# Modulation vectors computed in pairs over four blocks of partitions, with tied steps, in a FoX/GLA trunk

## The chip, the cores and the metric

The kernel runs on one core of one Trainium2 chip. The metric is the device time of one execution in microseconds (us). Times of single executions are given as the median, lowest and highest of several runs. The profile comes from one execution of its own, whose time is given beside the others. Engines are TensorE (PE, with its weight loads as PEld), VectorE (DVE), ScalarE (ACT), GpSimd (POOL) and SyncE (SP), whose queue starts nearly all the DMAs.

## What is computed

The reference is a trunk of two layers on a sequence of 1024 tokens with 1024 channels. Layer 0 mixes tokens with forgetting attention (FoX, 16 heads of 64 channels, softmax with a cumulative log gate), layer 1 with gated linear attention (GLA, 4 heads, chunks with a decayed state). Each mixer is followed by a SwiGLU feed-forward network (FFN) of width 2816. Before each of these four parts the stream is normalized and modulated by vectors that come from one conditioning vector c:

```python
    c_act = jax.nn.silu(c)
    for i in range(DEPTH):
        mod = c_act @ ada_w[i] + ada_b[i]
        sh1, sc1, g1, sh2, sc2, g2 = jnp.split(mod, N_MOD, axis=-1)
        h = modulate(rms_norm(x, norm1_g[i]), sh1, sc1)
        ...
        x = x + g1[:, None, :] * y
        h = modulate(rms_norm(x, norm2_g[i]), sh2, sc2)
        x = x + g2[:, None, :] * swiglu(h, ffn_w_in[i], ffn_w_out[i])
    return rms_norm(x, final_g)
```

The change is about the line with `mod`: for each layer a row vector of 1024 numbers times a matrix of 1024 rows and 6144 columns, cut into six vectors j = 0 to 5 of 1024 numbers. All data is float32.

## The kernel before, in words

**Products.** Each large product is made of three matmuls on parts: every operand is split into a high part, rounded to a short float (fp32r), and the rest, and high*high, high*low and low*high are summed in PSUM (`mm3`, L237 to L239). `split` (L159, L160) makes the parts: ACT copies the high part, DVE subtracts it. Weights come in by 512 KB DMAs into a ring `wr` of three slots (L162) and are split from there (`load_w`, L193 to L206). A `Weights` object loads a fixed number of weight tiles ahead. The FFN uses products of sums of blocks (a Strassen scheme), with sums on POOL (L683, L685) and DVE (L1285), and spills to device memory through SP.

**Order.** The program is written as one stream of instructions with data dependencies. A scheduler of the framework then sets the order on each engine, by its own estimate of durations, so an instruction without a reason to wait may move ahead of instructions written before it. `tc.issue_after(i)` ties the instructions issued under it behind instruction i. `weave` interleaves two generators by their estimated work: the attention steps of one head pair (`attention`, with the softmax in L902 to L962) with the projections of the next pair (`qk_proj`, and `v_half` for the value projection, whose weights are the tiles wv and whose PSUM tiles are vps).

**Modulation before.** At the start, vectors 0 and 1 of layer 0 come in eight slices of 128 columns (`load_ada0`, `ada0_mod`, L455 to L474), partly by matmuls, partly by DVE (L470) and a final matmul with a column of ones (L472). They feed the first normalized blocks (`h_block`, L476 to L484). The change leaves these alone. All the other vectors come from `ada_steps` (L336 to L383), one vector j at a time. Eight row blocks of 128 rows of `ada_w` are multiplied by their 128 numbers of silu(c), one for each partition, and added into `acc`. Eight (or, for a half vector, four) matmuls with `ones` (L377) then sum over the partitions, each giving a column of 128 numbers, DVE adds the bias from `vec` into `modc` (L379), and `make_a` (L333) makes the scale of the norm.

- *Layer 0, vectors 2 to 5*: a load of 512 KB (128 rows by 1024 columns) per step goes through the ring `wr` (L345), and four DVE instructions of 256 columns scale and add it (L367 for the first row block, L369 for the others). These steps are paced by `ada0(3.0)` after each `qk_proj` (L879).
- *Layer 1, all vectors*: half vectors, a load of 256 KB per step, always one step ahead; ACT scales (L358 for the first, L360 for the others) and POOL adds (L361). Vectors 0 and 1 run in the FFN of layer 0, paced by `ada1(...)` after its products (L1280), the others in GLA (after `gv_body`, and after the projections in `head_front`). The pace sets how much other work is written between steps (`ADA_A`, `ADA_B`).

**GLA gates.** `gate_z`, `gate_sum` and `gate_exps` make the decay factors of a head: two small matmuls (L1596, L1597), activations, two scans over the tokens on DVE (L1610), and exponentials. `head_front` makes the k and q projections of one head (PSUM tiles gk and gqp) and in between takes the two steps of `gate_ahead`, the same chain for the next head. In every head the steps were taken after the two halves of the k projection.

Of the kernel before, what the change touches and what calls it, by code (L numbers as in the profile page):

```python
# [16 lines left out]
P = 128  # L17
# [36 lines left out]
def trunk(ctx, tc, x, c, ada_w, ada_b, norm1_g, norm2_g, ffn_w_in, ffn_w_out,  # L54
# [98 lines left out]
    mhalf = cst.tile([P, 8], F32, name="mhalf")  # L153
    nc.vector.memset(mhalf, -0.5)
    maskb = cst.tile([P, P], BF16, name="maskb")
    tri = cst.tile([P, P], I32, name="tri")
# [123 lines left out]
    def load_ada0(d):  # L280
        for kh in range(2):
# [3 lines left out]
            araw[(d, kh)] = t  # L285

    load_x(0)
    rows2 = mrows[1][0:32]
# [26 lines left out]
    cact = cst.tile([P, 8], F32, name="cact")  # L315
    nc.scalar.activation(cact, vps[:, P:P + 8], AF.Silu)
    nc.vector.tensor_copy(vec, vps)
    gocol = lambda k: vec[:, P + 8 + k: P + 9 + k]
# [16 lines left out]

    def ada_steps(l, j, acc_of, raw_of, w):  # L336

        steps = deque((c0, k) for c0 in range(0, D, w) for k in range(8))
        got = deque()

        def load():
            if steps:
                c0, k = steps.popleft()
                raw = raw_of([P, w], F32, f"ada{l}{j}{c0}{k}")
                nc.sync.dma_start(raw, ada_w[l, psl(k), j * D + c0:j * D + c0 + w])  # L345
                got.append(raw)

        for c0 in range(0, D, w):
            acc = acc_of([P, w], F32, f"acc{l}{j}{c0}")
            for k in range(8):  # L350
                if w == D or c0 == k == 0:
                    load()
                raw = got.popleft()
                if w < D:
                    load()
                    yield ADA_A
                    if k == 0:
                        nc.scalar.mul(acc, raw, cact[:, 0:1])  # L358
                    else:
                        nc.scalar.mul(raw, raw, cact[:, k:k + 1])  # L360
                        nc.gpsimd.tensor_add(acc, acc, raw)  # L361
                    yield ADA_B
                    continue
                for q in range(0, w, 256):
                    cs = slice(q, q + 256)
                    if k == 0:
                        nc.vector.tensor_scalar(acc[:, cs], raw[:, cs], cact[:, 0:1], None, op0=ALU.mult)  # L367
                    else:
                        nc.vector.scalar_tensor_tensor(acc[:, cs], raw[:, cs], cact[:, k:k + 1], acc[:, cs],  # L369
                                                       op0=ALU.mult, op1=ALU.add)  # L370
                yield 1.0
            if w < D:
                yield ADA_B
            n, b = w // P, c0 // P
            mp = pj([P, n], F32, f"mp{l}{j}{c0}")
            for k in range(n):
                nc.tensor.matmul(mp[:, k:k + 1], acc[:, psl(k)], ones, start=True, stop=True)  # L377
            o = l * 48 + j * 8 + b
            nc.vector.tensor_add(modc[:, l, j, b:b + n], mp, vec[:, o:o + n])  # L379
            for i, jj in ((0, 1), (1, 4)):  # L380
                if j == jj:
                    make_a(l, i, slice(b, b + n))
        yield 1.0  # L383
# [24 lines left out]

    def ada1_queue(js, acc, raws_, w):
        r = Cycle(raws_)  # L410
        for j in js:
            ada1.q.append(ada_steps(1, j, lambda *_: acc, r, w))

# [576 lines left out]

    for j in (2, 3, 4, 5):
        ada0.q.append(ada_steps(0, j, acc_r, wr, D))
    run(v_half(0, 1))
# [522 lines left out]
    def mid0():  # L1516
        v = Views(slots["hid"], 2, [HALF], "ad0").v
        ada1_queue((0, 1), v[0], v[1:4], HALF)

# [22 lines left out]
    ada_v = Views(take(2), 2, [HALF], "ad").v  # L1542
    ada1_queue((2, 3, 4, 5), ada_v[0], ada_v[1:3], HALF)
    ADA_A, ADA_B = 2.5, 1.0
# [100 lines left out]
    def head_front(h, b16, t2, ei, nmid):  # L1645
# [4 lines left out]
        for hf in range(2):  # L1650
            cs = hsl(hf)
            ps = pj([P, HALF], F32, f"gk{h}{hf}")
            run(proj(ps, wk, h1, hf))
            ada1(5.1)
            y = yv()
            nc.vector.tensor_mul(y, ps, ei[:, cs])
            nc.vector.tensor_mul(t2[:, cs], ps, t2[:, cs])
            split(kin.hi[:, cs], kin.lo[:, cs], y)
            for n in range(4 * hf, 4 * hf + 4):
                nc.scalar.activation(ei[:, psl(n)], b16[:, psl(n)], AF.Exp, scale=1.0 / 16, bias=nmid[:, n:n + 1])  # L1660
            nc.scalar.activation(b16[:, cs], b16[:, cs], AF.Exp, scale=1.0 / 16)
            next(ahead, None)
        wq = feed.next()
        qt = [Pair(qr([P, S], FR, f"gq{h}{i}h"), qr([P, S], FR, f"gq{h}{i}l")) for i in range(2)]
        for hf in range(2):
            cs = hsl(hf)
            ps = pj([P, HALF], F32, f"gqp{h}{hf}")
            run(proj(ps, wq, h1, hf))
            ada1(5.1)
            for t, f in zip(qt, (ei, b16)):  # L1670
                y = yv()
                nc.vector.scalar_tensor_tensor(y, ps, QS, f[:, cs], op0=ALU.mult, op1=ALU.mult)
                split(t.hi[:, cs], t.lo[:, cs], y)
        return kin, qt

# [241 lines left out]
```

## Time and profile before

| | us |
|---|---|
| runs, median | 2447.19 |
| runs, lowest and highest | 2445.64, 2450.05 |
| profiled execution | 2444.76 |
| its span | 2443.0 |

The granted clock of PE over the profiled execution is 0.993 of full. The page of the profile gives, for each engine, busy time and share of the span; the view of waits says which instruction waited for which engine's tile or DMA; the timeline lists single instructions with their start, duration and, in brackets, the idle time of the engine ahead of them and what ended it; windows give busy times by stretches. Names are the program's, with numbers left out: `mp` is the PSUM tile of the modulation sums, `ad` and `ada` tiles are rows of `ada_w` (for layer 1 and 0), `adas` the slices at the start, `acc` the sums.

### The profile page before, as it was taken

The page shows a single profiled execution, that of the slowest core. Times are in us where ns is not written, and L with a number is a line of the kernel's source. Part 1 is how long each engine was busy: PE and PEld are TensorE (multiplying, and loading weights), DVE is VectorE, ACT ScalarE, POOL GpSimd, SP SyncE. Part 2 cuts the span into 40 slices and gives each one's busy share as a digit, 9 for nine tenths or more (in the row PEclk, how much of TensorE's full clock was granted, in tenths as well). Part 3 has the DMA queues.
Part 4 walks back from the last instruction along what each step waited for, and adds up shares of the span by engine and source line. Part 5 has one row for each costly group of instructions (what it writes and reads, how often), then busy time and mean ns, then how long its engine had stood idle before and what let it go on. Part 6 is the DMA issues. An engine that isn't in the chain of part 4 may idle for free.

```text
span 2443.0 us, 35539 instructions
## 1 busy us (share of the span) xinstructions
PE 2384.9 (98%) x12458; PEld 2028.7 (83%) x12458; DVE 1703.0 (70%) x2849; ACT 1192.8 (49%) x2280; POOL 1151.1 (47%) x1006
## 2 busy tenths in 40 slices
PE   6999999999999999999999899999999999999998
PEld 5788888878887878888888798898888888888888
DVE  6477777776687768675788456546487667665787
ACT  4565665665554443435324756654344333335325
POOL 4233333333348776653363544442326656653362
PEclk9999999999999999999999999999999999999999
DMA  8224333233326544347665333435325434347664
GB/s 269 80 87 121 96 96 120 70 96 113 128 94 212 183 164 164 125 162 261 228 215 178 92 114 111 125 107 169 107 73 191 147 134 155 130 166 257 232 209 149
DMA packets 319067, 362.34 MB, mean 148 GB/s; under 512 B 18140, under 2 KB 246648, under 8 KB 318888
## 3 DMA queue, kind: packets, MB, share of 16 engines
q1 hardware_dynamic: 318888, 360.07, 44.2%
q8 instruction: 98, 1.61, 0.3%
q14 instruction: 81, 0.66, 0.1%
HBM read 269.76 MB, written 90.24 MB: 147 GB/s over the span
## 4 chain that ended last, share of the span: by engine, by line
PE 82%; DVE 7%; DMA 3%; ACT 3%; issue 3%; POOL 2%; SPq 0%; DVEq 0%; POOLq 0%; ACTq 0%
PE p_b L237 15%; PE p_b L239 15%; PE p_b L238 14%; PE o_b L947 2%; PE t_b L933 2%; PE qk_b L237 2%; PE qk_b L238 2%; PE qk_b L239 2%; DMA ad_s<-in_ada_w_dram 1%; PE s_b L902 1%; PE s_b L903 1%; PE gv_b L237 1%; PE gv_b L239 1%; PE gv_b L238 1%; PE vps_b L237 1%
## 5 line engine op out<-in xcount | busy, mean ns | idle before, releaser
L160 DVE TENSOR_TENSOR o_s<-xv_s,o_s 128x512 fp32r<-128x512 f32 (+1 forms) x376 | 325.8, 870 | 90.3 <-ACT o_s L159 89.0
L159 ACT CAST o_s<-xv_s 128x512 fp32r<-128x512 f32 (+1 forms) x376 | 217.3, 586 | 307.2 <-PE p_b L239 257.7
L237 PE MATMUL p_b<-B,o_s 128*128 128x512 f32 x608 | 236.9, 392 | 6.5 <-DVE x L1285 4.1
L238 PE MATMUL p_b<-B,o_s 128*128 128x512 f32 x608 | 238.1, 392 | 0.0
L239 PE MATMUL p_b<-B,o_s 128*128 128x512 f32 x608 | 237.5, 391 | 0.0
L913 POOL TENSOR_SCALAR lp_s<-lp_s,st 128x128 f32<-128x128 f32 (+7 forms) x128 | 96.2, 756 | 294.2 <-DVE st L912 280.8
L683 POOL TENSOR_TENSOR ex_s<-xv_s,xv_s 128x512 f32<-128x512 f32 (+1 forms) x64 | 89.3, 1396 | 254.2 <-DMA xv_s<-in_ffn_w_in_dram 92.1
L237 PE MATMUL p_b<-T,o_s 128*128 128x512 f32 x480 | 187.4, 391 | 0.0
L238 PE MATMUL p_b<-T,o_s 128*128 128x512 f32 x480 | 186.8, 389 | 0.0
L239 PE MATMUL p_b<-T,o_s 128*128 128x512 f32 x480 | 182.0, 389 | 0.0
L237 PEld LDWEIGHTS p_b<-B,o_s 128*128 128x128 f32 x608 | 114.9, 189 | 31.6 <-DVE x L1285 3.4
L239 PEld LDWEIGHTS p_b<-B,o_s 128*128 128x128 f32 x608 | 114.9, 189 | 24.0
L238 PEld LDWEIGHTS p_b<-B,o_s 128*128 128x128 f32 x608 | 114.9, 189 | 23.7
L911 ACT ACTIVATE lp_s<-lp_s,st 128x128 f32<-128x128 f32 (+7 forms) x128 | 99.3, 776 | 56.4 <-DVE st L907 55.9
L1285 DVE TENSOR_TENSOR ex_s<-ex_s,p_b 128x512 f32<-128x512 f32 x140 | 94.0, 681 | 34.6 <-PE p_b L239 34.3
L159 ACT CAST pt_s<-t_b 128x512 fp32r<-128x512 f32 (+1 forms) x160 | 80.1, 547 | 71.5 <-PE t_b L933 70.5
L685 POOL TENSOR_TENSOR xv_s<-ex_s,xv_s 128x512 f32<-128x512 f32 (+1 forms) x64 | 84.0, 1312 | 62.5 <-DVE o_s L160 60.4
L160 DVE TENSOR_TENSOR pt_s<-t_b,pt_s 128x512 fp32r<-128x512 f32 (+1 forms) x160 | 96.5, 631 | 18.2 <-ACT pt_s L159 17.5
L239 PEld LDWEIGHTS p_b<-T,o_s 128*128 128x128 f32 x480 | 90.1, 188 | 18.9
L238 PEld LDWEIGHTS p_b<-T,o_s 128*128 128x128 f32 x480 | 90.1, 188 | 18.5
L237 PEld LDWEIGHTS p_b<-T,o_s 128*128 128x128 f32 x480 | 90.1, 188 | 18.5
L907 DVE CUSTOM_DVE_ANT_0 lp_s<-s_b,cum_s 128x512 f32<-128x512 f32 (+3 forms) x128 | 72.7, 570 | 41.7 <-PE t_b L933 22.9
(1947 smaller groups left out, 7543.4 us busy)
## 6 DMA issues: line engine op xcount, KB each, us to landing
xv_s<-in_ffn_w_in_dram SPq DMA_DIRECT2D x176, 256.0 KB, 3.0
hid_B<-x SPq DMA_DIRECT2D x70, 512.0 KB, 2.6
ad_s<-in_ada_w_dram SPq DMA_DIRECT2D x96, 256.0 KB, 2.9
hid_T<-x SPq DMA_DIRECT2D x36, 512.0 KB, 2.7
xv_s<-in_ffn_w_out_dram SPq DMA_DIRECT2D x96, 192.0 KB, 4.6
ada_s<-in_ada_w_dram SPq DMA_DIRECT2D x32, 512.0 KB, 3.8
xv_s<-in_ffn_w_out_dram SPq DMA_DIRECT2D x40, 256.0 KB, 2.8
T2o<-hid_T SPq DMA_DIRECT2D x18, 512.0 KB, 8.5
```

What stands on the lines that cost most here:

```text
L159: nc.scalar.copy(hi, src)
L160: nc.vector.tensor_sub(lo, src, hi.bitcast(F32))
L237: nc.tensor.matmul(ps, ah, bh, start=start, stop=False)
L238: nc.tensor.matmul(ps, ah, bl, start=False, stop=False)
L239: nc.tensor.matmul(ps, al, bh, start=False, stop=stop)
L683: nc.gpsimd.tensor_add(s1, a21, a22)
L685: nc.gpsimd.tensor_sub(a11, s1, a11)
L907: nc.vector.tensor_tensor_reduce(lp[:, k0:k1], ps, cm[:, k0:k1], 1.0, mcur, ALU.add, ALU.min, mnew)
L911: nc.scalar.activation(lp, lp, AF.Exp, bias=mcur, scale=-1.0, accum_out=st[:, qi, 2:3])
L913: nc.gpsimd.tensor_scalar(lp, lp, st[:, qi, 3:4], 1.0, op0=ALU.mult, op1=ALU.mult)
L933: nc.tensor.transpose(tp[:, i, :], lps[qi][:, psl(2 * b + jj)], ident)
L1285: nc.vector.tensor_add(d, d if src is None else dest(G, src), ps)
```

## The change

`ada_steps` becomes `ada_pair`, which takes two vectors at once. The 2048 columns of a pair are cut into four blocks of 512, and each block has 32 partitions: partition 32q + r holds block q of row 32r + s in step s, so 32 steps s cover the 1024 rows and `acc` is 128 by 512. A step is loaded by four DMAs, one for each block of 32 partitions: 64 KB each in layer 1 (one row per partition), 128 KB each in layer 0 (two rows per partition, n = 2). The numbers of silu(c) for this layout are `cblk`, loaded by four small DMAs on ACT's queue and made by one more activation. The sum over partitions takes four matmuls with four columns each, against `quart`, whose column q is one on block q and zero elsewhere; one DVE instruction adds the bias for the pair. Ten vectors become five pairs.

Each scaling instruction is tied by `issue_after` behind the last instruction of its own engine written so far: ACT's in layer 1, DVE's in layer 0. DMAs, POOL's adds and the matmuls are not tied.

The counts over the kernel: `mp` matmuls on PE 80 before and 20 after; DMAs of these weights on SP 128 and 512, of the same 40 MB; DVE's scaling steps 128 and 128; ACT's 96 and 96; POOL's adds 84 and 93.

Apart from this, `head_front` takes the two steps of `gate_ahead` after the halves of the q projection in head 0, and as before after those of the k projection in the other heads.

```diff
--- before.py
+++ after.py
@@ -152,6 +152,10 @@
     nc.vector.memset(ones, 1.0)
     mhalf = cst.tile([P, 8], F32, name="mhalf")
     nc.vector.memset(mhalf, -0.5)
+    quart = cst.tile([P, 4], F32, name="quart")
+    nc.vector.memset(quart, 0.0)
+    for q in range(4):
+        nc.vector.memset(quart[32 * q:32 * q + 32, q:q + 1], 1.0)
     maskb = cst.tile([P, P], BF16, name="maskb")
     tri = cst.tile([P, P], I32, name="tri")
 
@@ -284,6 +288,10 @@
                 nc.sync.dma_start(t[:, :, j, :], adaw[0, :, 4 * kh:4 * kh + 4, j, d, :])
             araw[(d, kh)] = t
 
+    craw = mrows[4][:, 0:32]
+    cblk = cst.tile([P, 32], F32, name="cblk")
+    for q in range(4):
+        nc.scalar.dma_start(craw[32 * q:32 * q + 32], c[0].rearrange("(r s) -> r s", s=32))
     load_x(0)
     rows2 = mrows[1][0:32]
     nc.vector.memset(rows2, 0.0)
@@ -314,6 +322,7 @@
     vec = cst.tile([P, 160], F32, name="vec")
     cact = cst.tile([P, 8], F32, name="cact")
     nc.scalar.activation(cact, vps[:, P:P + 8], AF.Silu)
+    nc.scalar.activation(cblk, craw, AF.Silu)
     nc.vector.tensor_copy(vec, vps)
     gocol = lambda k: vec[:, P + 8 + k: P + 9 + k]
     fgcol = lambda k: vec[:, P + 20 + k: P + 21 + k]
@@ -333,53 +342,61 @@
         nc.vector.scalar_tensor_tensor(amul[:, l, i, ks], modc[:, l, j, ks], 1.0,
                                        vec[:, g0:g0 + 8][:, ks], op0=ALU.add, op1=ALU.mult)
 
-    def ada_steps(l, j, acc_of, raw_of, w):
-
-        steps = deque((c0, k) for c0 in range(0, D, w) for k in range(8))
+    def last_of(e):
+        return next(i for i in reversed(nc.cur_bb.bb.instructions) if i.engine == ENG[e])
+
+    def ada_pair(l, j, acc_of, raw_of, n):
+
+        steps = deque(range(0, 32, n))
         got = deque()
+        rows_ = ada_w[l, :, j * D:(j + 2) * D].rearrange("(r s) (q m) -> q r s m", s=32, q=4)
 
         def load():
             if steps:
-                c0, k = steps.popleft()
-                raw = raw_of([P, w], F32, f"ada{l}{j}{c0}{k}")
-                nc.sync.dma_start(raw, ada_w[l, psl(k), j * D + c0:j * D + c0 + w])
-                got.append(raw)
-
-        for c0 in range(0, D, w):
-            acc = acc_of([P, w], F32, f"acc{l}{j}{c0}")
-            for k in range(8):
-                if w == D or c0 == k == 0:
-                    load()
-                raw = got.popleft()
-                if w < D:
-                    load()
-                    yield ADA_A
-                    if k == 0:
-                        nc.scalar.mul(acc, raw, cact[:, 0:1])
+                s = steps.popleft()
+                raw = raw_of([P, n * HALF], F32, f"ada{l}{j}{s}")
+                for q in range(4):
+                    nc.sync.dma_start(raw[32 * q:32 * q + 32].rearrange("r (s m) -> r s m", s=n),
+                                      rows_[q, :, s:s + n])
+                got.append((s, raw))
+
+        acc = acc_of([P, HALF], F32, f"acc{l}{j}")
+        for i in range(0, 32, n):
+            if n > 1 or i == 0:
+                load()
+            s0, raw = got.popleft()
+            if n == 1:
+                load()
+                yield ADA_A
+                with tc.issue_after(last_of("A")):
+                    if i == 0:
+                        nc.scalar.mul(acc, raw, cblk[:, 0:1])
                     else:
-                        nc.scalar.mul(raw, raw, cact[:, k:k + 1])
-                        nc.gpsimd.tensor_add(acc, acc, raw)
-                    yield ADA_B
-                    continue
-                for q in range(0, w, 256):
-                    cs = slice(q, q + 256)
-                    if k == 0:
-                        nc.vector.tensor_scalar(acc[:, cs], raw[:, cs], cact[:, 0:1], None, op0=ALU.mult)
-                    else:
-                        nc.vector.scalar_tensor_tensor(acc[:, cs], raw[:, cs], cact[:, k:k + 1], acc[:, cs],
-                                                       op0=ALU.mult, op1=ALU.add)
-                yield 1.0
-            if w < D:
+                        nc.scalar.mul(raw, raw, cblk[:, i:i + 1])
+                if i:
+                    nc.gpsimd.tensor_add(acc, acc, raw)
                 yield ADA_B
-            n, b = w // P, c0 // P
-            mp = pj([P, n], F32, f"mp{l}{j}{c0}")
-            for k in range(n):
-                nc.tensor.matmul(mp[:, k:k + 1], acc[:, psl(k)], ones, start=True, stop=True)
-            o = l * 48 + j * 8 + b
-            nc.vector.tensor_add(modc[:, l, j, b:b + n], mp, vec[:, o:o + n])
-            for i, jj in ((0, 1), (1, 4)):
-                if j == jj:
-                    make_a(l, i, slice(b, b + n))
+                continue
+            tie = last_of("D")
+            for s in range(s0, s0 + n):
+                for c0 in range(0, HALF, 256):
+                    cs, rs_ = slice(c0, c0 + 256), slice((s - s0) * HALF + c0, (s - s0) * HALF + c0 + 256)
+                    with tc.issue_after(tie):
+                        if s == 0:
+                            nc.vector.tensor_scalar(acc[:, cs], raw[:, rs_], cblk[:, 0:1], None, op0=ALU.mult)
+                        else:
+                            nc.vector.scalar_tensor_tensor(acc[:, cs], raw[:, rs_], cblk[:, s:s + 1], acc[:, cs],
+                                                           op0=ALU.mult, op1=ALU.add)
+            yield 1.0
+        if n == 1:
+            yield ADA_B
+        mp = pj([P, 16], F32, f"mp{l}{j}")
+        for b in range(4):
+            nc.tensor.matmul(mp[:, b:16:4], acc[:, psl(b)], quart, start=True, stop=True)
+        o = l * 48 + j * 8
+        nc.vector.tensor_add(modc[:, l, j:j + 2, :].rearrange("p j k -> p (j k)"), mp, vec[:, o:o + 16])
+        if j in (0, 4):
+            make_a(l, j // 4)
         yield 1.0
 
     class Pace:
@@ -406,10 +423,10 @@
 
     ada0, ada1 = Pace(), Pace()
 
-    def ada1_queue(js, acc, raws_, w):
+    def ada1_queue(js, acc, raws_):
         r = Cycle(raws_)
         for j in js:
-            ada1.q.append(ada_steps(1, j, lambda *_: acc, r, w))
+            ada1.q.append(ada_pair(1, j, lambda *_: acc, r, 1))
 
     mk = mrows[2]
     nc.vector.memset(mk, 0.0)
@@ -988,8 +1005,8 @@
         for g in gs:
             yield from g
 
-    for j in (2, 3, 4, 5):
-        ada0.q.append(ada_steps(0, j, acc_r, wr, D))
+    for j in (2, 4):
+        ada0.q.append(ada_pair(0, j, acc_r, wr, 2))
     run(v_half(0, 1))
     for p in range(7):
         parts = [qk_proj(p + 1, 0), qk_proj(p + 1, 1)]
@@ -1515,7 +1532,7 @@
 
     def mid0():
         v = Views(slots["hid"], 2, [HALF], "ad0").v
-        ada1_queue((0, 1), v[0], v[1:4], HALF)
+        ada1_queue((0,), v[0], v[1:4])
 
     ADA_A, ADA_B = 6.0, 3.0
     ffn(0, oh, xs, slots, "fo", mid0, norm_mixer)
@@ -1540,7 +1557,7 @@
     athl = Ring(big, take(1))
     s_slot, on_slot = take(2)
     ada_v = Views(take(2), 2, [HALF], "ad").v
-    ada1_queue((2, 3, 4, 5), ada_v[0], ada_v[1:3], HALF)
+    ada1_queue((2, 4), ada_v[0], ada_v[1:3])
     ADA_A, ADA_B = 2.5, 1.0
     rm = ada_v[3]
     nc.vector.memset(rm, 1.0)
@@ -1659,7 +1676,8 @@
             for n in range(4 * hf, 4 * hf + 4):
                 nc.scalar.activation(ei[:, psl(n)], b16[:, psl(n)], AF.Exp, scale=1.0 / 16, bias=nmid[:, n:n + 1])
             nc.scalar.activation(b16[:, cs], b16[:, cs], AF.Exp, scale=1.0 / 16)
-            next(ahead, None)
+            if h:
+                next(ahead, None)
         wq = feed.next()
         qt = [Pair(qr([P, S], FR, f"gq{h}{i}h"), qr([P, S], FR, f"gq{h}{i}l")) for i in range(2)]
         for hf in range(2):
@@ -1671,6 +1689,8 @@
                 y = yv()
                 nc.vector.scalar_tensor_tensor(y, ps, QS, f[:, cs], op0=ALU.mult, op1=ALU.mult)
                 split(t.hi[:, cs], t.lo[:, cs], y)
+            if not h:
+                next(ahead, None)
         return kin, qt
 
     last_og = deque()
```

## The prediction

> **What bounds the kernel now.** I read the page first: shares of busy time, then the chain that ended last.
>
> ```profile
> span 2443.0 us, 35539 instructions
> PE 2384.9 (98%) x12458; PEld 2028.7 (83%) x12458; DVE 1703.0 (70%) x2849; ACT 1192.8 (49%) x2280; POOL 1151.1 (47%) x1006
> ...
> PE 82%; DVE 7%; DMA 3%; ACT 3%; issue 3%; POOL 2%; SPq 0%; DVEq 0%; POOLq 0%; ACTq 0%
> ```
>
> TensorE is busy for 2384.9 of 2443.0 us. So an edit pays in two ways only: fewer or faster matmuls, or less of the 58 us in which PE is idle. No other engine is full; DVE, ACT, POOL and SP count only where PE waits for them. The view of the waits of PE shows where that is:
>
> ```profile
> PE mp_b L472 <- DVE acc L470: 6.6, 2, 5.3
> ...
> PE gk_b L237 <- DVE modc L379: 4.6, 1, 4.6
> PE p_b L237 <- DVE x L1285: 4.1, 2, 3.0
> ...
> PE p_b L237 <- DVE sg_s L1285: 2.4, 1, 2.4
> ```
>
> The columns are the sum in us, the number of waits and the longest. The change touches the cause of all four: the first stands behind modulation work on DVE, the second is a modulation vector itself, the others follow an ACT queue that waits for modulation weights. The four sum to 17.7 us.
>
> **Part 1: the reductions on PE.** Each vector was summed over partitions by 8 matmuls with one column. Ten vectors make 80; the trace holds two records for each.
>
> ```profile
> L377 PE MATMUL mp_b<-ones,ad_s 128*128 128x1 f32 x96 | 11.7, 233 | 0.0
> L377 PE MATMUL mp_b<-ones,acc_s 128*128 128x1 f32 x64 | 8.2, 236 | 0.0
> ```
>
> ```profile
> 181.19 0.95 PE L377 MATMUL mp_b<-ones,acc_s 128*128 128x1 f32 x8
> 182.00 0.53 PE L933 MATMUL t_b<-ident,lp_s 128*128 128x128 f32 x3
> ```
>
> Four matmuls (8 records) hold PE from 181.19 to 182.00, 0.81 us, or 0.20 us each: 80 x 0.20 = 16 us. The changed kernel has five pairs of four matmuls with four columns: 20 x 0.20 = 4 us. **-12 us.** By the busy sums, (11.7 + 8.2)/80 = 0.249 us each, it is 60 x 0.249 = -14.9. The four-column form is not in the trace; the nearest rows are these and the 128x128 matmul beside them (0.53 us for three records), so I take no difference, and -10 as the poor end.
>
> **Part 2: the start.** Layer 0's vectors 2 to 5 were taken up by DVE whenever it came free. Some of that floated ahead of startup work that PE waits for.
>
> ```profile
> 54.00:66.00 12.00, 3.59 (x17) 2.55 (x16) 10.93 (x17) 2.55 (x4) 8.98 (x10) 0.69 0.16 47
> 66.00:80.00 14.00, 14.00 (x79) 12.43 (x78) 9.13 (x17) 10.71 (x19) 2.58 (x2) 0.90 0.50 149
> ```
>
> ```profile
> 56.43 0.33 PE L479 MATMUL xp_b<-ident,xt_s 128*128 128x128 f32 x1 [1.34 <-POOL xt_s L450]
> 57.69 0.33 PE L479 MATMUL xp_b<-ident,xt_s 128*128 128x128 f32 x1 [0.92 <-POOL xt_s L450]
> 63.29 0.98 PE L472 MATMUL mp_b<-ones,acc 128*128 128x1 f32 x4 [5.28 <-DVE acc L470]
> ```
>
> ```profile
> 56.57 1.21 DVE L367 TENSOR_SCALAR acc_s<-ada_s,cact 128x256 f32<-128x256 f32 x1
> 57.70 1.33 DVE L470 SCALAR_TENSOR_TENSOR acc<-adas_s,cact,acc 128x256 f32<-128x256 f32 x1
> 58.95 3.20 DVE L367 TENSOR_SCALAR acc_s<-ada_s,cact 128x256 f32<-128x256 f32 x3
> ...
> 62.67 0.47 DVE L470 SCALAR_TENSOR_TENSOR acc<-adas_s,cact,acc 128x256 f32<-128x256 f32 x1
> ```
>
> The windows' columns are PE, PEld, DVE, ACT and POOL busy, then granted clock, DMA share, GB/s. PE works 3.59 of 12 us, while the last L470, for which it waits 5.28 us, stands behind four L367 of the next vector: 1.21 + 3.20 = 4.4 us. The ties forbid that: in the changed kernel's order no such step stands ahead of the first scores, and POOL takes one of its h0l tiles ahead of the scaling of xt. I count -4.4 for DVE, -2.3 for the two POOL waits (1.34 + 0.92), and -1.4 for the clock after the long gap (14 us at 0.90 instead of 1.00). **-8 us**; -10 if all goes, -4 if only the L367 go.
>
> **Part 3: the start of attention, where the ties cost.** Now these steps stand behind score work on DVE, and until they run they hold slots of the three-slot ring through which wv, w_ and ada tiles all come. The loads of wv on SP:
>
> ```profile
> 64.76 0.38 SPq L194 DMA_DIRECT2D wv_s<-in_fox_w_in_dram  x1
> ...
> 72.56 0.38 SPq L194 DMA_DIRECT2D wv_s<-in_fox_w_in_dram  x1
> ```
>
> a matmul of PE that uses its second half, and a block of steps on DVE at that time:
>
> ```profile
> 127.64 0.28 PE L237 MATMUL vps_b<-wv_0h_s,h0h 128*128 128x256 f32 x1
> ```
>
> ```profile
> 126.73 2.77 DVE L369 SCALAR_TENSOR_TENSOR acc_s<-ada_s,cact,acc_s 128x256 f32<-128x256 f32 x4
> ```
>
> Before, wv was issued by 73 us, and such vps_b matmuls filled PE while it would have waited for softmax. In the changed kernel's order one stretch early in attention has 40 matmuls of scores, transposes and outputs and no projection among them, since wv comes only after the tied steps have freed two slots. There PE sees the passage of the softmax through the other engines, of which the page has the parts:
>
> ```profile
> L913 POOL TENSOR_SCALAR lp_s<-lp_s,st 128x128 f32<-128x128 f32 (+7 forms) x128 | 96.2, 756 | 294.2 <-DVE st L912 280.8
> ...
> L911 ACT ACTIVATE lp_s<-lp_s,st 128x128 f32<-128x128 f32 (+7 forms) x128 | 99.3, 776 | 56.4 <-DVE st L907 55.9
> ...
> L159 ACT CAST pt_s<-t_b 128x512 fp32r<-128x512 f32 (+1 forms) x160 | 80.1, 547 | 71.5 <-PE t_b L933 70.5
> ...
> L160 DVE TENSOR_TENSOR pt_s<-t_b,pt_s 128x512 fp32r<-128x512 f32 (+1 forms) x160 | 96.5, 631 | 18.2 <-ACT pt_s L159 17.5
> ...
> L907 DVE CUSTOM_DVE_ANT_0 lp_s<-s_b,cum_s 128x512 f32<-128x512 f32 (+3 forms) x128 | 72.7, 570 | 41.7 <-PE t_b L933 22.9
> ```
>
> One passage is 0.57 + 0.78 + 0.76 + 0.55 + 0.63 = 3.3 us. The stretch has two in sequence, and a block of steps in the DVE queue (2.77 us for four) delays them once more, by a third or so, 0.9: 2 x 3.3 + 0.9 = **+7.5 us**. One passage alone is +3, three with a whole block +12.
>
> **Part 4: FFN of layer 0.** Here ACT scales the rows for layer 1. Before, these stand bunched, and ACT waits for their loads ahead of work that PE needs.
>
> ```profile
> ACT ad_s L360 <- DMA ad_s<-in_ada_w_dram: 32.4, 21, 5.2
> ```
>
> ```profile
> 745.06 0.72 ACT L360 ACTIVATE ad_s<-ad_s,cact 128x512 f32<-128x512 f32 x1 [2.49 <-DMA ad_s<-in_ada_w_dram]
> ```
>
> ```profile
> 746.10 0.50 PE L237 MATMUL p_b<-B,o_s 128*128 128x512 f32 x1 [2.96 <-DVE x L1285]
> ```
>
> The first is ACT's waits between 725 and 960 us: 32.4 us on these loads, reaching PE as the 4.1 + 2.4 = 6.5 us of L1285. With each scale tied behind the last ACT instruction written, they stand about evenly, 6 to 12 instructions apart, and a load has a step's time to land. I take **-5 us**; -6.5 if all goes, -1 if ACT waits as before. The number of scales (96) stays, and POOL gets nine adds more.
>
> **Part 5: GLA.** A modulation add stands behind two scans on DVE while its PSUM bank keeps gk_b from starting.
>
> ```profile
> 1385.49 3.28 DVE L1610 TENSOR_TENSOR_SCAN b_s<-ad_s,t_s 128x512 f32<-128x512 f32 x2
> 1388.70 0.13 DVE L379 TENSOR_TENSOR modc<-mp_b,vec 128x4 f32<-128x4 f32 x1
> ```
>
> ```profile
> 1388.00:1390.00 2.00, 1.12 (x3) 0.93 (x4) 1.79 (x6) 0.98 (x4) 0.00 (x0) 0.50 0.27 93
> 1390.00:1392.00 2.00, 2.00 (x6) 1.55 (x5) 0.70 (x2) 2.00 (x9) 0.00 (x0) 0.50 0.00 0
> 1392.00:1394.00 2.00, 2.00 (x8) 1.60 (x7) 0.59 (x1) 2.00 (x8) 0.00 (x0) 0.71 0.00 0
> ...
> 746.00:748.00 2.00, 1.90 (x8) 1.58 (x9) 0.20 (x2) 2.00 (x5) 0.00 (x0) 1.00 1.04 351
> ```
>
> The wait is 4.6 us, and then the clock is 0.50 for 3.1 us and 0.71 for 2: 1.6 + 0.6 = 2.2 us lost. Both go, since no reduction stands there any more: -6.8. But the gate chain of head 0 now steps after the q projection, so its scans are late for whatever uses a bank or a decay next; the same kind of wait for a scan of 1.6 us (3.28 for two) can come back, and I charge +2.8. **-4 us**, from -7 to +1.
>
> The Trainium skill, in "TensorE: Matmul & The Clock Gate", Part 1: The HAM clock gate, has the array fall to half clock after an idle window of about 3.4 us. The trace agrees: 0.50 after gaps of 4.6 and 5.28 us, 1.00 after 2.96. By that page each of the two long gaps that goes takes a slow spell with it, and the sum above already has that from the rows.
>
> **Part 6: small things.** Memsets, four tiny loads on ACT's queue and a silu at the start lie beside the first loads of weights; four DMAs stand where one was.
>
> ```profile
> 775.32 0.41 SPq L345 DMA_DIRECT2D ad_s<-in_ada_w_dram  x1
> ```
>
> ```profile
> SPq L345 <- POOL ad_s L361: 135.0, 71, 9.0
> ```
>
> At 0.41 us three more issues put 1.2 us on SP per step, 384 x 0.41 = 157 us in all, but SP already waits 135 us for POOL to free these very buffers, and its next loads are not what PE waits for in the view of waits. **+1 us**, 0 to +2.
>
> **Sum:** -12 - 8 + 7.5 - 5 - 4 + 1 = -20.5 us against the profiled execution, 2444.76 us (span 2443.0 and 1.8 around it). The median of the runs, 2447.19, is 2.4 above that execution, so I give 2444.76 - 20.5 + 2.4 = **2426.7 us**.
>
> **Rivals.** (A) *Weights late all through attention; slower.* If the ring is held not once but at every batch of tied steps, each batch costs a stretch like Part 3's, 7.5 us. The other terms give -28, so from four stretches (30) it is slower; with five, -28 + 37.5 = +9.5, 2457 us. For it: 16 steps of two rows share three slots with all weights. Against: in the changed order all later stretches without projections are shorter than the first, and no longer than before's longest. 0.13.
>
> (B) *Four issues for one undo the spacing.* If the last of four pieces lands as late as the bunched loads did, ACT waits on as before, Parts 4 and 5 give nothing, and only -12 - 8 + 7.5 + 1 = -11.5 is left: 2436 us. For it: the DMA share of 1.04 at 746 us. Against: the bytes are the same. 0.17. The Trainium skill, in "DMA: Bandwidth & Descriptors", Rules for kernel authors, says that transfers under 64 KB are mostly overhead and that two transfers to disjoint partitions serialize; the layer-1 pieces, 64 KB, sit at that limit. No run here shows the split form yet.
>
> (C) *The new stretch gates the clock.* A single idle of over 4 us in Part 3 costs a slow spell of 2.2 us, two of them 4.4: 2431 us. For it: a passage of 3.3 with a block of 2.77 behind it is 6.1. Against: two blocks of scores are in flight. 0.10.
>
> **How the numbers follow.** Forecast 0.60, A 0.13, B 0.17, C 0.10. Faster or slower than 0.2%, 4.9 us, is about what a measurement of this kernel can tell from no change. The forecast's own ends, not all at once, give 2414 to 2440; A's reach beyond is partly taken in: **2413 to 2445**. Of A, 0.11 is slower and 0.02 the same; of B 0.12 faster, 0.04 same, 0.01 slower; of C 0.09 faster, 0.01 same; of the forecast 0.59 faster, 0.01 same. Faster 0.80, same 0.08, slower 0.12.
>
> **What would show it.** Right: 40 reduction records on PE for 160; no wait of over 2 us for L470; PE idle without projections at 110 to 150 us; no wait on modc in GLA; ACT's waits on ad_s in the FFN well below 32.4 us. Wrong: PE waits for split weights at several places in 120 to 500 us (A), or those ACT waits unchanged (B).

## The result, and the profile after

The changed kernel takes 2452.3 us (median of 20 runs, 2446.47 to 2455.55), the kernel before 2447.09 us in the same series. The ratio is 1.0017, with a 95% interval of 1.001 to 1.0023. So it is slower by 0.17%, just inside the 0.2% below which the prediction says "same", where the forecast was 2426.7 us. The profiled execution took 2448.36 us, at the quick end of its runs: 3.9 us below their median, and 3.6 us above the profiled execution of before. The profiles of the experiments below lie within 1.5 us of their medians, so against the changed kernel each of them stands some 2 to 5 us lower by the medians than by the profiles.

The page of the changed kernel shows that the first aim was met, PE has less to do, and that it did not help:

```profile
span 2446.5 us, 36077 instructions
...
PE 2379.8 (97%) x12338; PEld 2021.2 (83%) x12338; DVE 1713.7 (70%) x2841; ACT 1189.5 (49%) x2281; POOL 1169.6 (48%) x1015
```

PE is busy for 5.1 us less (2384.9 before), yet the span grew by 3.5. To see where, I compared the start of the same matmul in both timelines at four places. The kernel before:

```profile
96.40 0.40 PE L492 MATMUL fs_b<-h0l,fw_s 128*128 128x512 f32 x1
...
533.17 0.47 PE L237 MATMUL fo000p_b<-ohh,wo_0h_s 128*128 128x512 f32 x1
...
1283.15 0.47 PE L237 MATMUL f0e01800p_b<-hh,oo_s 128*128 128x512 f32 x1 [0.27 <-issue]
...
1687.29 0.39 PE L237 MATMUL go000p_b<-ghh,wo_0h_s 128*128 128x512 f32 x1
```

The changed kernel, whose last fs_b matmul starts 8.0 us earlier than before:

```profile
88.44 0.40 PE L509 MATMUL fs_b<-h0l,fw_s 128*128 128x512 f32 x1
...
547.30 0.48 PE L241 MATMUL fo000p_b<-ohh,wo_0h_s 128*128 128x512 f32 x1
...
1284.93 0.47 PE L241 MATMUL f0e01800p_b<-hh,oo_s 128*128 128x512 f32 x1 [0.31 <-issue]
...
1689.38 0.39 PE L241 MATMUL go000p_b<-ghh,wo_0h_s 128*128 128x512 f32 x1
```

These are the end of the start (fs_b), the first product after attention (fo000p), the last block of layer 0's FFN (f0e) and the first product after GLA (go000p). Against before the changed kernel is at -8.0, +14.1, +1.8, +2.1 and, at the end of the span, +3.5 us. So: **start -8.0, attention +22.1, output and FFN -12.4, GLA +0.3**, and 1.4 behind that. Two large gains are there; attention gives them back.

PE's waits in the changed kernel have new names:

```profile
PE gqp_b L241 <- DVE gy_s L1690: 5.1, 1, 5.1
PE o_b L964 <- DVE pt_s L164: 4.9, 8, 1.0
PE o_b L964 <- DVE oT_s L979: 4.7, 4, 1.8
PE t_b L950 <- POOL lp_s L930: 4.6, 2, 4.2
```

The old ones on modc and x are gone, and 0.4 us is left of the one on acc. The attention stage, from the last fs_b matmul to the first of fo000p, as one window, before and then after (PE, PEld, DVE, ACT, POOL busy, clock, DMA share, GB/s):

```profile
96.40:533.17 436.77, 428.16 (x2813) 376.98 (x2812) 325.03 (x852) 269.61 (x577) 156.79 (x217) 1.00 0.31 97
```

```profile
88.44:547.30 458.86, 435.31 (x2777) 379.44 (x2776) 335.99 (x866) 269.71 (x577) 161.60 (x217) 0.97 0.33 96
```

The stage is 22.1 us longer. PE's idle time in it grew from 8.6 to 23.6 us, +14.9, and its busy time by 7.2 us, although 24 fewer reductions at 0.2 us should take 4.8 off; so the other matmuls take some 12 us more, beside a clock of 0.97 (0.03 x 459 = 14). The chain through 97 to 530 us of the changed kernel goes first of all through the modulation steps of DVE (L388), which carry 9.0% of it, 39 us:

```profile
by line: DVE acc_s L388 9.0%; PE o_b L964 8.3%; PE t_b L950 8.2%; PE qk_b L241 8.0%; PE qk_b L242 7.6%; PE qk_b L243 7.4%; DVE lp_s L924 5.7%; issue 4.3%; PE s_b L919 3.9%; DVE pt_s L164 3.8%; PE s_b L920 3.6%; PE vps_b L241 2.9%; PE vps_b 
```

### The profile page after: what moved, and what is told of

It is laid out like the page before. It is cut to its first block, busy times and chain, and to the rows that moved or that the text cites. A ratio compares the mean times of both kernels' runs of the same rounds, so it can differ in the third digit from the quotient of the medians.

```text
span 2446.5 us, 36077 instructions
## 1 busy us (share of the span) xinstructions
PE 2379.8 (97%) x12338; PEld 2021.2 (83%) x12338; DVE 1713.7 (70%) x2841; ACT 1189.5 (49%) x2281; POOL 1169.6 (48%) x1015
## 4 chain that ended last, share of the span: by engine, by line
PE 78%; DVE 8%; DMA 4%; ACT 3%; issue 2%; SPq 2%; POOL 2%; DVEq 0%; POOLq 0%; ACTq 0%
PE p_b L243 15%; PE p_b L242 15%; PE p_b L241 15%; PE o_b L964 2%; PE t_b L950 2%; DVE acc_s L388 2%; PE qk_b L241 1%; PE qk_b L242 1%; PE qk_b L243 1%; PE gr_b L241 1%; PE gr_b L243 1%; DVE lp_s L924 1%; PE gr_b L242 1%; DMA ad_s<-in_ada_w_dram 1%; PE s_b L919 1%
## 5 line engine op out<-in xcount | busy, mean ns | idle before, releaser
L164 DVE TENSOR_TENSOR o_s<-xv_s,o_s 128x512 fp32r<-128x512 f32 (+1 forms) x376 | 339.3, 906 | 83.9 <-ACT o_s L163 83.2
L377 POOL TENSOR_TENSOR ad_s<-ad_s,ad_s 128x512 f32<-128x512 f32 x53 | 80.7, 1523 | 62.8 <-ACT ad_s L375 38.0
L964 PE MATMUL o_b<-pt_s,v_s 128*128 128x256 f32 x512 | 97.2, 301 | 12.7 <-DVE pt_s L164 4.9
```

What stands on the lines that cost most here:

```text
L164: nc.vector.tensor_sub(lo, src, hi.bitcast(F32))
L964: nc.tensor.matmul(ops, lv, pts[b][:, hl, 2 * jj:2 * jj + 2, :], start=j == 0 and hl == 0, stop=False)
```

## The experiments

Theory T: the ties of layer 0 make the loss, because a tie releases a block of DVE steps behind the newest work, in the way of the softmax. Rivals: S, only the late value weights at the start of attention; L, the layout with four DMAs for one. Ratios are to the kernel before, with 95% intervals. The table gives each profile against the profile of before, in us, by stage, from the same matmuls as above. Stages that an edit does not touch differ between profiles by 3 to 4 us, and GLA by up to 6: e10, whose edit is in attention, has -4.6 there and e6 +1.4.

| | start | attention | output, FFN | GLA | median us | ratio |
|---|---|---|---|---|---|---|
| changed kernel | -8.0 | +22.1 | -12.4 | +0.3 | 2452.30 | 1.0017 (1.001 to 1.0023) |
| e1 untied | -0.5 | +2.2 | -9.6 | +1.0 | 2437.53 | 0.9962 (0.9948 to 0.9977) |
| e2 one tie | -7.8 | +8.9 | -9.2 | -2.4 | 2434.67 | 0.9943 (0.9924 to 0.9963) |
| e3 later | -8.2 | +16.3 | -12.6 | 0.0 | 2441.56 | 0.9974 (0.9962 to 0.9985) |
| e4 gate back | -7.7 | +21.8 | -9.3 | -4.2 | 2443.69 | 0.9981 (0.9968 to 0.9994) |
| e6 later, untied | -8.4 | +0.4 | -11.0 | +1.4 | 2429.18 | 0.9928 (0.9909 to 0.9947) |
| e7 as e6, gate back | -8.5 | -0.6 | -12.2 | -2.0 | 2423.84 | 0.9898 (0.9872 to 0.9923) |
| e8 layer 1 untied | -7.4 | +25.6 | +9.5 | +6.2 | 2479.54 | 1.0129 (1.011 to 1.0148) |
| e10 smaller blocks | -7.6 | +8.1 | -9.4 | -4.6 | 2434.23 | 0.9938 (0.9915 to 0.9961) |
| e11 before, ACT tied | +2.2 | -1.1 | -8.0 | +3.9 | 2444.39 | 0.9986 (0.9973 to 0.9999) |
| e12 as e7, repeated | -7.3 | +0.6 | -10.4 | -5.0 | 2422.99 | 0.9901 (0.9878 to 0.9923) |

**e1: layer 0 untied.**

```diff
-                    with tc.issue_after(tie):
+                    if True:
```

> The changed kernel with layer 0's scaling steps on DVE no longer tied (pairs, loads and layer 1 as changed). In the profiles the changed kernel gains 8.0 us on the old one up to 97 us, then loses 22.1 us in attention, so that it is 14.1 us behind at 530 us. Theory T (the ties make the loss: steps stand late and in blocks in DVE's queue, and hold load slots and POOL meanwhile): most of the 22 us go, and 5 or so of the start come back as loss; 10 to 18 us below the changed kernel, near 2438 us, a few us below the kernel before. Rival L (the layout of pairs makes it: four DMAs per load, 32 rows per DMA): within 4 us of the changed kernel, near 2452.

It came out at 2437.53 us. Of the 22.1 us in attention 19.9 went, and 7.5 of the start came back. T holds, L falls: with the same layout and the same four DMAs attention is within 2.2 us of before.

**e2: one tie for all.**

```diff
-            tie = last_of("D")
+            tie = vars(ada_pair).setdefault("tie", last_of("D"))
```

> All of layer 0's DVE steps are tied to one instruction, the one that the first step was tied to (the query rows of head pair 1), instead of each to the last one written. Theory T, in the form that each later tie costs: the first loss of about 10 us up to 150 us stays, the next 12 us up to 460 us go; 8 to 14 us below the changed kernel. If only the start of attention mattered (rival S, wv late once), within 3 us of the changed kernel. Rival L: within 3 us too; e1 tells S and L apart.

It came out at 2434.67 us. Attention lost 8.9 us instead of 22.1, with the start kept. The first loss stayed, the later one went, so 13 us were from the ties after the first. S as the only cause falls.

**e3: the pairs two projections later.**

```diff
-    run(v_half(0, 1))
+    ada0.at = -6.0; run(v_half(0, 1))
```

> The ties stay, but layer 0's pairs begin two projections later (pace set to -6 at first), so that no row of ada_w holds a slot of the ring when the value weights of the second half load. Rival S (late value weights): the 10 us of the first loss go, to 2442. Theory T: the blocks of steps only move; the first loss comes 25 us later or is spread, and the total is within 4 us of the changed kernel.

It came out at 2441.56 us, 10.7 below the changed kernel, which is what S said; T's 4 us were missed. The first loss went: at 154 us this kernel is still 8 us ahead of before. But between 277 and 532 us it then lost 14 us, which S alone does not explain, and in the profiles attention loses only 5.8 us less than in the changed kernel. With e2: both the missing fill at the start and the blocks later on are real.

**e10: smaller blocks.**

```diff
-            (k_evac if i else q_evac)(ps, qkt[p], hf)
-        ada0(3.0)
+            (k_evac if i else q_evac)(ps, qkt[p], hf); ada0(1.5)
```

> As the changed kernel, but layer 0's pace is called with 1.5 after each half of a projection instead of 3.0 after both, so a tie releases 8 or 16 DVE steps at a time instead of 24; each step is still tied behind the last DVE instruction written. If the size of the blocks makes the loss in attention (22.1 us between 97 and 530 us in the profile): 6 to 12 us below the changed kernel. If the loss is that steps run late and hold load slots, whatever their grouping: within 4 us of it.

More than expected: 18 us below the changed kernel, and attention loses 8.1 us instead of 22.1. The counts in the expectation are twice too high: a load is four DVE instructions and a call takes three loads (four the first time), so the changed kernel's blocks are of 12 instructions (16 the first, 8 at the end of a pair), and those of e10 of 4 or 8. The same steps are tied to newer work each time. So the release of three loads at a time makes the larger part of the loss.

That does not say by which way. Three loads are also all the slots of the ring, through which the weights come. The waits of the weight loads on SP for these steps, in attention, in the kernel before, the changed kernel and e10:

```profile
SPq L194 <- DVE acc_s L369: 29.1, 12, 4.0
```

```profile
SPq L198 <- DVE acc_s L388: 137.0, 19, 22.5
```

```profile
SPq L198 <- DVE acc_s L388: 35.0, 9, 8.5
```

It is 154.7 us in e3, and 32.2 in e2 and 21.6 in e1. Wherever the later loss stands, the ring is held as well. No run ties such blocks and leaves the ring free, so how much of the loss comes from DVE's queue and how much from later weights is not separated.

**e5 and e9: is POOL kept out by DVE?** In the changed kernel PE's longest new wait in attention is on POOL. The three timelines, of DVE, POOL and PE, and two windows:

```profile
120.46 2.83 DVE L388 SCALAR_TENSOR_TENSOR acc_s<-ada_s,cblk,acc_s 128x256 f32<-128x256 f32 x7
```

```profile
120.12 4.17 POOL L930 TENSOR_SCALAR lp_s<-lp_s,st 128x1024 f32<-128x1024 f32 x1 [5.25 <-DVE st L929]
```

```profile
124.34 2.18 PE L950 MATMUL t_b<-ident,lp_s 128*128 128x128 f32 x9 [4.17 <-POOL lp_s L930]
```

```profile
120.00:124.00 4.00, 0.17 (x2) 0.00 (x0) 3.30 (x11) 0.01 (x1) 3.88 (x1) 0.50 0.55 145
124.00:128.00 4.00, 3.66 (x17) 3.46 (x17) 2.10 (x5) 2.62 (x5) 1.77 (x4) 0.50 0.74 250
```

Seven DVE steps run from 120.46 to 123.29 without a gap. A POOL scaling that was released at 120.12 is through only about 1 us after them, PE stands still, and its clock is 0.50 in both windows. Elsewhere in this kernel a scaling of this size takes 1.1 to 1.3 us. Two small kernels tried the pair of them alone. The heart of the second, with the kinds of DVE step in `step` left out:

```python
    for k, kind in enumerate(("two", "one", "ts", "psum")):
        ...
        dve(lambda: nc.vector.tensor_copy(r[:, k:k + 1], gate[:, k:k + 1]))
        nc.gpsimd.tensor_scalar(lp[k], lp[k], r[:, k:k + 1], 1.0, op0=ALU.mult, op1=ALU.mult)
        for i in range(16):
            step(k, i, kind)
```

> A kernel of its own that computes nothing of the reference: four POOL tensor_scalar instructions of 128x1024 (the form of the softmax scaling) alone; 24 DVE scale-and-add instructions of 128x256 alone with both inputs in SBUF (the form of the modulation steps); the two together; POOL beside 24 DVE tensor_scalar with one SBUF input; POOL beside 24 scale-and-adds whose second input and output are in PSUM. In the changed kernel one POOL scaling took 4.17 us while ten such DVE steps ran, against 1.17 us mostly. If DVE's two-input form keeps POOL out: alone 1.1 to 1.2 us on POOL, beside it 3 to 12 us for the first, and near 1.2 beside the PSUM form. If the 4.17 us had another reason: 1.2 us in all sections.

Four scalings took 4.6 us alone (1.12, 1.12 and 2.37 for two), 5.12 us beside the two-input form, 4.58 beside the one-input form and 4.41 beside the PSUM form. The two-input DVE steps went from 485 ns alone to 608 ns.

> Again a kernel of its own that computes nothing of the reference. Each section has three DVE steps of 128x256, a 128x1 copy on DVE that lets one POOL scaling of 128x1024 start, and then sixteen more DVE steps. Section 1: scale-and-add with both inputs in SBUF on two accumulators in turn, as the changed kernel has them; 2: on one accumulator (each step needs the one before, as in e5); 3: tensor_scalar with one SBUF input; 4: scale-and-add with the accumulator in PSUM. If a dense block of two-input steps that has already begun keeps POOL out until its end: the one POOL scaling takes 7 to 9 us in section 1 (it waits for 16 steps of 0.4 to 0.5 us) and 1.1 to 1.3 us in sections 3 and 4; 2 tells whether the gap between dependent steps lets POOL in. If not: near 1.2 us in all four, and the 4.17 us of the changed kernel stay unexplained.

The timelines of e9, DVE in section 1 and POOL in sections 1 and 4:

```profile
5.46 7.29 DVE L69 SCALAR_TENSOR_TENSOR acc<-raw,gate,acc 128x256 f32<-128x256 f32 x16
```

```profile
5.60 1.33 POOL L81 TENSOR_SCALAR lp<-lp,r 128x1024 f32<-128x1024 f32 x1 [5.16 <-DVE r L80]
...
33.25 1.12 POOL L81 TENSOR_SCALAR lp<-lp,r 128x1024 f32<-128x1024 f32 x1 [6.22 <-DVE r L80]
```

POOL took 0.2 us longer, not 7. In e5 it was DVE that lost more, 24 x 0.12 = 3.0 us against 0.5. So a dense block does not by itself keep POOL out, and the single long scaling in the changed kernel is not explained; it also stands in e2, e4 and e8 (4.17 us each), is 2.19 us in e10, and is missing in e1, e3 and e6, where no scaling takes over 1.3 us. The Trainium skill, in "SBUF — State Buffer", SBUF: two separate sides, says that a DVE instruction with two inputs in SBUF and a POOL instruction that reads SBUF shut each other out for a whole instruction. The trace agrees for single instructions: beside a POOL scaling one L388 of the changed kernel takes 1.28 us where its neighbour takes 0.47. Whether a whole block can hold POOL off like that stays open: e9 was built to show it and does not.

```profile
261.94 1.93 POOL L930 TENSOR_SCALAR lp_s<-lp_s,st 128x1024 f32<-128x1024 f32 x2 [2.95 <-PE s_b L922]
```

```profile
261.69 0.47 DVE L388 SCALAR_TENSOR_TENSOR acc_s<-ada_s,cblk,acc_s 128x256 f32<-128x256 f32 x1
...
262.14 1.28 DVE L388 SCALAR_TENSOR_TENSOR acc_s<-ada_s,cblk,acc_s 128x256 f32<-128x256 f32 x1
```

**e8 and e11: the ties of layer 1.** e8 unties the changed kernel, e11 ties the kernel before.

```diff
-                with tc.issue_after(last_of("A")):
+                if True:
```

> Layer 1's scales on ACT untied, all else as changed. In the profiles the changed kernel gains 12.2 us on the old one in the FFN of layer 0 (from +14.0 at 669 us to +1.8 at 924), of which some 5 us are the 24 reduction matmuls that are left out. Theory: the ties make the other 7 us; then this kernel is 5 to 9 us above the changed one, about 2459. Rival: the loads a step ahead and the fewer vectors make it; within 3 us of the changed kernel.

It is 27 us above the changed kernel, three times what was expected (of the reductions left out, 12 and not 24 are in the FFN). In the profiles 22 us of it lie in the FFN. ACT's waits between 660 and 960 us and a window in e8:

```profile
ACT ad_s L375 <- DMA ad_s<-in_ada_w_dram: 28.8, 16, 4.0
```

```profile
750.00:800.00 50.00, 41.99 (x169) 32.71 (x168) 34.93 (x36) 23.80 (x40) 42.90 (x30) 0.94 0.72 219
```

The old wait of ACT for modulation rows is back (32.4 us before), and PE idles 8 us in 50. In the changed kernel ACT waits for no row there, and PE does not idle at all in the FFN's middle:

```profile
726.00:960.00 234.00, 234.00 (x1034) 193.78 (x1033) 186.67 (x210) 102.33 (x176) 180.56 (x117) 1.00 0.54 175
```

> The kernel before, with one edit: each scaling of layer 1 on ACT is tied behind the last ACT instruction written. Single vectors, 256 KB loads and reductions stay. e8 showed that without the ties the new layout loses 27 us against the changed kernel, with ACT waiting 28.8 us for ada rows in the FFN. Theory: the ties take away the ACT waits in the old layout as well; 4 to 10 us below the kernel before, all of it between 700 and 900 us. Rival: the ties help only the new layout, whose 64 KB loads land later; within 3 us.

```diff
...
+                    with tc.issue_after(next(i for i in reversed(nc.cur_bb.bb.instructions) if i.engine == ENG["A"])):
+                        nc.scalar.mul(raw if k else acc, raw, cact[:, k:k + 1])
...
```

In its profile the FFN gains 8.0 us in the old layout as well, and PE's idle time there falls from 7.6 to 0.8 us, so the ties do it and not the pairs. But the kernel as a whole gains only 2.5 us at the median, 0.14%: by the time alone that is where the rival put it, and the theory's 4 us were missed. In the profile GLA loses 3.9 us, within what GLA differs by between profiles.

**e4, e6, e7, e12: the gate chain, and a quicker version.**

```diff
-            if h:
+            if True:
                 next(ahead, None)
...
-            if not h:
+            if False:
                 next(ahead, None)
```

> Head 0's gate steps go back behind the halves of the k projection; all else as changed. In the changed kernel GLA gains 8 us by 1394 us and gives it back by 1412, in a wait of 5.1 us on gqp with half clock behind it. Theory: that wait comes from the moved gate chain, and the old wait on the k projection came from a reduction of a vector that no longer stands there; then the move is undone for a gain of 3 to 8 us. Rival: the wait of 4.6 us on gk comes back in the place of the one on gqp; within 3 us.

The median fell by 8.6 us against the changed kernel, and e7 against e6 has a gain again, of 5.3 us at the median. Neither theory nor rival had the wait right: none came back on gk, and the one on gqp stayed, at 6.3 us. Where the gain comes from is not shown: GLA is 4.5 us shorter in the profile, but in e10, which has the gate chain of the changed kernel, it is 4.9 shorter too.

e6 has the edits of e1 and e3 together; e7 and e12 have that of e4 as well.

> Layer 0's steps untied and begun two projections later. e1 showed the ties to cost 19 us in attention but to save 8 us at the start, e3 that the later beginning takes the first 10 us away. If the start is saved because no row of ada_w is loaded before the value weights, this has both: about -8 at 97 us and near -6 at 530 us against the kernel before, in all 18 to 24 us below the changed kernel, 2428 to 2434. If only ties keep the start free: as e1, 2438.

2429.18 us: the start keeps its 8 us without a tie, since no row of ada_w is loaded that early, and attention is within 0.4 us of before.

> As e6, with the gate steps of head 0 back behind the k projection. e4 put that at 8.6 us in the medians, 4 to 5 in the profile between 1329 and 1700 us. If the two are independent: 4 to 8 us below e6, 2422 to 2428; if e4's gain was chance, within 2 us of e6.

> The kernel of e7 again with more rounds, for the size of its gain: 2424 us there, 0.990 of the kernel before (0.987 to 0.992). Expected 2422 to 2426.

2423.84 us, and 2422.99 in the repeat (ratio 0.9901, 0.9878 to 0.9923). This kernel has the pairs, layer 1's ties, untied steps of layer 0 that begin two projections later, and the gate chain where it was. It beats both, by 1% against before.

## Why the prediction was wrong

**The reductions: right.** The four-column matmuls cost what the others did:

```profile
L395 PE MATMUL mp_b<-quart,ad_s 128*128 128x4 f32 x24 | 2.8, 242 | 0.0
L395 PE MATMUL mp_b<-quart,acc_s 128*128 128x4 f32 x16 | 1.9, 242 | 0.0
```

20 matmuls take 4.7 us by the busy sums, 0.235 each against 0.249; 60 fewer were counted as -12. PE's busy time over the kernel fell by 5.1 us only, as in attention it grew by 7.2.

**The start: right, its exact size by luck.** -8 was forecast, -8.0 came. PE's waits on L470 and on POOL's xt fell by 8.5 us, where 6.7 had been counted, and its busy time by 3.2 at a better clock (0.98 against 0.93), where 1.4 had been; other waits grew by 3.7, which had not been counted, and that brings it back to -8. I put the gain down to the ties, and e1, with the loads early and no ties, loses it. But e6 has no ties there and keeps it: it is enough that no row is loaded and ready before the first normalized blocks are done.

**The start of attention: the step that failed.** Part 3 charged +7.5 us for one stretch without projections, with the ties on either side of it as free. With the reductions that is a net +2.7 for attention; it was +22.1. The stretch is there and costs some 9 us (e2 keeps it, e3 is without it). Rival C's single long idle is part of it: PE waits 4.17 us, with the clock at 0.50. The rest, 13 us, is the term that I left out: each later call of the pace releases three loads under ties, 12 DVE instructions of 0.53 us, or 6.4 us of DVE work, all behind the newest instruction written for DVE. Before, these ran wherever DVE was free. A block in the changed kernel, and PE at its end:

```profile
238.30 1.67 DVE L388 SCALAR_TENSOR_TENSOR acc_s<-ada_s,cblk,acc_s 128x256 f32<-128x256 f32 x4
239.89 0.16 DVE L929 RECIPROCAL st<-st 128x1 f32<-128x1 f32 x1
239.96 0.47 DVE L388 SCALAR_TENSOR_TENSOR acc_s<-ada_s,cblk,acc_s 128x256 f32<-128x256 f32 x1
...
243.66 0.94 DVE L388 SCALAR_TENSOR_TENSOR acc_s<-ada_s,cblk,acc_s 128x256 f32<-128x256 f32 x1
244.63 0.42 DVE L979 TENSOR_TENSOR oT_s<-o_b,ot 64x256 f32<-64x256 f32 x1
```

```profile
245.10 1.43 PE L964 MATMUL o_b<-pt_s,v_s 128*128 128x256 f32 x5 [1.75 <-DVE oT_s L979]
```

From 234.19 to 245.06 us DVE hardly pauses, with 12 L388 among the instructions of the softmax, and PE waits for DVE. Seven of the eight blocks of 12 have such waits of PE for DVE within 4 us of their end, 11.4 us together, and three spells of half clock begin there (near 200, 245 and 378 us). The amount of DVE work is not the reason: DVE works 11 us longer in the stage than before (335.99 us against 325.03), 16 of the steps having come over from the start, but it works as long in e10 (336.88 us), which loses 8.1. I looked for stretches in PE's order and found one, and took every later tie as free. Rival A had the right place, every batch. Its cause, a ring held at every batch, is there as well (137.0 us of waits on SP), but no wait of PE names a weight; how much of the 13 us it makes is open, as said at e10.

**The FFN: right, too small.** -5 and 2.4 for 12 reductions were forecast, -12.4 came. PE's idle time in the stage fell from 7.6 to 1.3 us, and all of its wait on L1285 went, about the -6.5 that Part 4 kept for its best case; e8 and e11 show that the ties did it. PE's busy time fell by 6.1 us, where 2.4 had been counted. Rival B, four DMAs undoing the spacing, did not happen: ACT waits for no row in the FFN.

**GLA: wrong.** -4 and -4.8 for 24 reductions were forecast, +0.3 came. The wait on modc went and one of 5.1 us on gqp took its place, 14 us later, with half clock in it and behind it. The timeline of PE and windows of the changed kernel:

```profile
1402.46 0.80 PE L241 MATMUL gqp_b<-h1h,w_h_s 128*128 128x512 f32 x1 [5.12 <-DVE gy_s L1690]
```

```profile
1398.00:1400.00 2.00, 0.00 (x0) 0.00 (x0) 1.15 (x3) 2.00 (x5) 1.59 (x3) 0.57 0.42 105
1400.00:1402.00 2.00, 0.00 (x0) 0.00 (x0) 1.52 (x3) 2.00 (x6) 2.00 (x3) 0.50 0.16 36
...
1406.00:1408.00 2.00, 2.00 (x6) 1.57 (x5) 0.00 (x0) 1.97 (x3) 1.27 (x1) 0.50 0.44 115
```

ACT is busy for all of 1398 to 1402 us: PE has run out of work while ACT makes, among other things, the exponentials of the first head. A wait of this size stands on gqp in every profile in which the one on gk is gone, also where the gate chain was not moved (6.3 us in e4, 6.8 in e11). So the +2.8 that I charged for a wait that comes back was right in that one came, wrong in its reason, the moved gate chain, and about a third of its price: 5.1 us and some 3 of slow clock. As this stage differs by up to 6 us between profiles, the +0.3 is not exact either.

The Trainium skill, in "TensorE: Matmul & The Clock Gate", Part 1: The HAM clock gate, has the half clock after idle windows of about 3.4 us. The clock is 0.50 behind the waits of 4.17 and 5.12 us, but the trace does not agree on the length: a mean of 0.57 in 1398 to 1400 us is 0.50 for 1.7 of these 2 us, so the clock fell near 1398.3, when PE had waited 0.9 us, with one wait of 1.04 us just before. In the kernel before it had fallen 2.1 us into the wait of 4.6 (0.59 in 1386 to 1388 us). And it fell at a wait of 1.75 us that ended at 245.10:

```profile
244.00:246.00 2.00, 0.90 (x4) 0.90 (x5) 1.91 (x7) 0.74 (x2) 0.32 (x1) 0.65 0.31 78
246.00:248.00 2.00, 2.00 (x9) 1.71 (x9) 1.96 (x4) 1.07 (x4) 0.00 (x0) 0.50 0.58 227
```

In this kernel, then, waits well below 3.4 us cost clock as well, which neither Part 3 nor rival C counted.

**The sum.** Forecast -20.5; in the profiles +3.6, by the medians +5.2. Attention is off by 19.4 us, GLA by 9.1, the FFN by -5.0. That the gains elsewhere nearly cancel the loss is chance.

## What to carry to other kernels

A tie to the last instruction written keeps work from floating ahead of what matters, but it also makes it as late as it can be, all at once: count how many instructions are released at once, put them beside the chain that uses the same engine, and ask which buffers they hold until then. When work floats too early, starting its loads later can do the same without ties, as in e6. A wait that is removed where an engine has run out of work comes back at the next place: ask what the other engines have still to do by then.

## What the runs showed that was not expected

In the profiles, ties on ACT were worth 22 us in the FFN with the new layout and 8 with the old; why untied steps of the new layout cost more, with no longer waits of ACT for rows (28.8 us against 32.4), is not shown. Beside a dense block of DVE steps, a POOL scaling took 1.33 us in a kernel with nothing else and once 4.17 us in the changed kernel; the reason of the latter stays open. In every profile of the changed layout, PE's wait on gqp is 5.1 us with the gate chain moved and 6.3 us with it where it was.
